# An encoder kernel on Trainium2: layer 1's gate projection by Strassen's seven block products

## The chip, the cores and the metric

The kernel runs on one core of one Trainium2 chip. A core has five engines that run side by side, each with its own queue of instructions: TensorE (PE, matrix products; its weight loads are listed apart as PEld), VectorE (DVE), ScalarE (ACT), GpSimd (POOL) and SyncE (SP, which here only issues DMAs). Data lies in DRAM, in SBUF (128 partitions) and in PSUM, into which TensorE writes. The metric is the device time of one execution in microseconds (us), and the median of several runs counts. The profile shows one execution.

## The reference: what is computed

A two-layer encoder on x of 1024 tokens x 1024 features, float32. Layer 0 is differential attention, layer 1 multi-head latent attention; the change touches layer 1. Each layer does

```python
h = _rmsnorm(x, norm_g[i]) * (1.0 + scale) + shift      # shift, scale, gate = silu(c) @ ada_w + ada_b
x = x + gate * y
```

and layer 1's `y`, with one input projection of 384 + 256 + 64 + 1024 columns, is

```python
proj = h @ w_in
q_a, c_kv, k_pe, z = jnp.split(proj, [384, 640, 704], axis=-1)
q = (_rmsnorm(q_a, q_a_norm_g) @ w_q_b)                  # 8 heads x (128 + 64)
kv = (_rmsnorm(c_kv, kv_a_norm_g) @ w_kv_b)              # 8 heads x (128 key + 128 value)
k_pe = _rope(k_pe, positions)
...                                                      # softmax attention per head
o = o.reshape(b, s, MLA_WIDTH) * jax.nn.silu(z)
return o @ w_out
```

`z`, the gate path, is the part whose matrix product changes: 1024 tokens x 1024 features by 1024 x 1024 weights. `q_a` (384 wide) and `c_kv` (256 wide) are the latents.

## The kernel before

**Numbers in two parts.** TensorE is fed a reduced float32 type (`F32R`). To keep float32 accuracy every operand is held as a high part (a rounded copy) and a low part (what is left), and each product is three matmuls into one PSUM bank (`mm3`, L177: high x high L178, high x low L179, low x high L180). An operand tile is 128x512; splitting one is a ScalarE copy and a GpSimd subtraction (`split_raw`, L214, lines L223 and L224, tiles `wh` and `wl`).

**Layer 1's input projection.** Its input h1 is kept transposed: 8 chunks of 128 features (`h1[k]`), each in two halves of 512 tokens, high and low. `group0` (L1166) makes them from the residual rows: transposes on TensorE, the high part on ScalarE, a float32 copy in a temporary and the low part on VectorE (`h_chunk`, L473). The projection is made in strips of 128 output columns. A strip is 2 halves x 8 chunks x 3 matmuls, and its weights are two 256 KB loads, each split in `split_raw`.

- Strip 0 is k_pe, with its rotation (`rope`, `kp_half`).
- Strips 1 to 3 are q_a, strips 4 and 5 c_kv (`lora`, L1223). `put` copies each half out of PSUM (`craw`), squares it (`csq`) and adds the squares up (`csum`, L1237). `norm` brings the sums onto partitions, takes the root on GpSimd (`rq_y`) and sends it through DRAM to all partitions (`bc_s`). `rest` scales (VectorE, L1251), copies the high part (ScalarE, L1254) and subtracts (GpSimd, L1255) into the tiles CQ and CK, which stay in SBUF until attention has used them.
- Strips 6 to 13 are z, one for each head (`z1_strip`, L1282). `silu_gate` (L701) makes z·(1 + tanh(z/2)) straight from PSUM, and the result goes to DRAM (`zS`).

Beside the z strips the modulation's gate of layer 1 is made: `gen_gate` (L438) loads eight 512 KB rows and reduces each in one VectorE operation (L428, in `mod_dot`). In the last z strip `load_wk` (L1304) loads and splits the value weights. Then `v1_tile` (L1314) makes the first half of the values, `store_v` (L353) splits each out of PSUM (L355 ScalarE, then VectorE) into one of three `v_hl` tiles and stores it (`vS`), and then `Stream` (L296) makes the heads' keys and queries (`kn`, `qn`, `qp`) from CK and CQ ahead of and beside attention (`attn1`, L1404).

**What sets the order.** Each engine runs its instructions in one fixed order. A planner chooses it when the program is built: instructions are taken in program order as far as what they need is thought to be ready. Python's order thus matters, and so do the lists that spread work: `Side` (L275) runs one entry at each tick, a tick being one chunk of a strip's loop, `norms` runs what is due at chunk `NORM_AT` = 4 of a half-strip, and `behind` ties an instruction to a place. Tiles with the same tag share buffers, and a new tile waits for the one that it replaces.

Of the kernel before, what the change touches and what calls it, by code (L numbers as in the profile page):

```python
# [78 lines left out]
def f32v(ap):  # L79
    return ap.bitcast(F32)  # L80
# [3 lines left out]
def trunk(ctx: ExitStack, tc: tile.TileContext, A, out):  # L84
# [388 lines left out]
    def h_chunk(l, xn4, k, dst, hp, sub=G, wide=False, act=False):  # L473
# [12 lines left out]
        tmp = hp.tile([P, n, P], F32, name="h32", tag="h32", bufs=2)  # L486
# [674 lines left out]
    w4 = []  # L1161
# [4 lines left out]
    def group0(gi, fulls):  # L1166
# [3 lines left out]
        def chunk(k):  # L1170
            if gi == 1:
                h1[k][1] = xt2k("h1h"), xt2k("h1l")
            h_chunk(1, fulls, k, h1[k][gi], p3x, V)
# [3 lines left out]
        side.add(*[lambda k=k: chunk(k) for k in range(KT)])  # L1177
# [13 lines left out]
    cqp = pool(stC, "cq", side="right")  # L1191
    CQ = [[(cqp.tile([P, HF], F32R, name=f"cqh{k}_{f}"), cqp.tile([P, HF], F32R, name=f"cql{k}_{f}")) for f in range(2)] for k in range(3)]
    CK = [[(cqp.tile([P, HF], F32R, name=f"ckh{k}_{f}"), cqp.tile([P, HF], F32R, name=f"ckl{k}_{f}")) for f in range(2)] for k in range(2)]
# [4 lines left out]
    st4 = ExitStack()  # L1198

    def kp_half(half, acc):  # L1200
        rot, fin = rope(wp, acc, half, 1.0)

        def g():
            rot()
            r = fin()
            hi = lr.tile([P, HF], F32R, name="kp_h", tag="kp_h", bufs=1)
# [5 lines left out]

    norms = []

    def half_and_norm(w, half, consume):

        for k, _ in enumerate(gen_half(w, h1, half, consume)):
            if k == NORM_AT:
                for f in norms[:]:
                    norms.remove(f)  # L1220
                    f()

    def lora(idx, dst, gvec, width, ws=None, first=None):  # L1223
# [3 lines left out]
        def put(i, half, acc):  # L1227
            t = lr.tile([P, HF], F32, name="craw", tag="craw", bufs=6)
# [5 lines left out]
            else:  # L1234
                s2 = lr.tile([P, HF], F32, name="csq", tag="csq", bufs=1)
# [3 lines left out]
        def norm(half):  # L1239
# [6 lines left out]
            _, rb = bcast_rows(lr, y, "cbc", 1)  # L1246

            def rest():
                for i in range(n):
# [3 lines left out]
                    hi, lo = dst[i][half]  # L1253
                    S.copy(hi, t)  # L1254
                    G.tensor_sub(lo, t, f32v(hi))  # L1255

            norms.append(rest)
# [11 lines left out]
    def first_halves(put):  # L1269

        g0 = kp_half(0, strip_half(w4[0], h1, 0))
# [3 lines left out]
        st3x.close()  # L1275
        g0()
        kp_half(1, strip_half(w4[0], h1, 1))()

    lora((1, 2, 3), CQ, qag, QL, w4[1], first_halves)
    lora((4, 5), CK, kvg, KVL)  # L1280

    def z1_strip(h, extra=None):  # L1282
        w = strip1(6 + h)
        if extra:
            extra()
        for half in range(2):
            def put(acc, half=half):
                gz = silu_gate(wp, acc)
# [338 lines left out]
```

## Time and profile before

| what | value |
| --- | --- |
| median of 3 runs | 1453.14 us (1454.03, 1447.42, 1453.14) |
| profiled execution | 1448.22 us |
| its span, first to last instruction | 1446.4 us |
| mean granted TensorE clock | 0.995 |
| instructions | 20456 |
| DMA traffic | 203.19 MB, mean 140 GB/s |
| z strips | 858.03 to 949.23 us of the span |

How to read it: busy time is the time in which an engine worked on instructions, and idle time of an engine that is not the bottleneck costs nothing. A row of a group gives line, engine, operation, output <- inputs, shapes and count, then busy us and mean ns of one, then the engine's idle us ahead of these and what ended it. A row of the timeline gives start, duration, engine, line and operation, with the idle time before it in brackets. A granted clock of 1.00 is TensorE's full speed.

### The profile page before, as it was taken

Reading aid. Unit: us, or ns where it says so; the run is one execution under the profiler, and the core shown is the slowest. Engines: PE = TensorE matmul, PEld = TensorE weight load, DVE = VectorE, ACT = ScalarE, POOL = GpSimd, SP = SyncE. Lnnn points to the kernel's source line nnn. Section 1 sums busy time; section 2 is a strip of 40 time slices with the busy share of each in tenths; the row PEclk is TensorE's granted clock in tenths of the full one; section 3 lists DMA queues with packets and bytes.
Section 4 is the critical chain, followed back from the end, with each engine's and each line's share of the span. In section 5 each row is a group of like instructions: output and inputs, shape, how many; then the busy total and the mean of one; then the engine's idle time right before and its main releaser. Section 6 shows DMA issues by size and latency. Waiting matters only on the chain.

```text
span 1446.4 us, 20456 instructions
## 1 busy us (share of the span) xinstructions
PE 1396.9 (97%) x7424; PEld 1167.0 (81%) x7424; DVE 858.4 (59%) x1272; ACT 710.5 (49%) x1258; POOL 605.0 (42%) x484
## 2 busy tenths in 40 slices
PE   5999999999999999998999999998999999999997
PEld 4778788888888887887787878787888888888886
DVE  6656777767777767677344445134555555555365
ACT  5522366656565665566343332234454554545342
POOL 4416164656564655453551264321141321412473
PEclk9999999999999999999999999999999999999999
DMA  9787823333333324137653127367242332345574
GB/s 327 234 248 234 256 66 97 87 103 81 101 97 88 98 81 110 63 95 262 229 171 124 38 69 239 110 189 204 77 104 77 110 99 76 105 136 175 172 238 149
DMA packets 128470, 203.19 MB, mean 140 GB/s; under 512 B 18289, under 2 KB 55281, under 8 KB 128369
## 3 DMA queue, kind: packets, MB, share of 16 engines
q1 hardware_dynamic: 128368, 201.89, 45.6%
q8 instruction: 58, 0.95, 0.3%
q14 instruction: 44, 0.35, 0.1%
HBM read 132.68 MB, written 45.56 MB: 123 GB/s over the span
## 4 chain that ended last, share of the span: by engine, by line
PE 77%; DMA 7%; DVE 6%; ACT 3%; POOL 3%; issue 2%; SPq 2%; ACTq 0%; DVEq 0%; POOLq 0%
PE s L1397 10%; PE acc L180 8%; PE acc L179 8%; PE acc L178 8%; PE tr L376 7%; PE s L767 7%; PE pv L179 4%; PE pv L178 4%; PE pv L180 4%; PE oacc L178 4%; PE oacc L179 4%; PE oacc L180 4%; DMA ada<-in_ada_g 2%; DMA wvr<-in_w_v 2%; DMA vS<-v_hl 1%
## 5 line engine op out<-in xcount | busy, mean ns | idle before, releaser
L378 ACT CAST pth<-tr 128x512 fp32r<-128x512 f32 x256 | 150.3, 587 | 283.6 <-PE tr L376 280.0
L393 DVE TENSOR_REDUCE nm<-s 128x1 f32<-128x1024 f32 x192 | 234.0, 1219 | 73.6 <-PE s L767 64.0
L379 DVE TENSOR_TENSOR ptl<-tr,pth 128x512 fp32r<-128x512 f32 x256 | 176.2, 688 | 150.2 <-ACT pth L378 149.9
L224 POOL TENSOR_TENSOR wl<-wraw,wh 128x512 fp32r<-128x512 f32 (+2 forms) x94 | 116.8, 1244 | 243.4 <-ACT wh L223 216.2
L395 ACT ACTIVATE e<-s,nm 128x1024 f32<-128x1024 f32 x128 | 143.7, 1122 | 28.1 <-DVE nm L393 27.6
L376 PE MATMUL tr<-ident,e 128*128 128x128 f32 x1024 | 154.6, 273 | 1.9 <-DVE ptl L379 1.7
L376 PEld LDWEIGHTS tr<-ident,e 128*128 128x128 f32 x1024 | 121.5, 140 | 42.8 <-DVE ptl L379 19.2
L178 PE MATMUL acc<-h0h,wh 128*128 128x512 f32 x360 | 150.0, 417 | 2.0 <-DVE v_hl L356 1.9
L178 PE MATMUL pv<-pth,vt 128*128 128x256 f32 x512 | 147.4, 288 | 0.0
L179 PE MATMUL pv<-ptl,vt 128*128 128x256 f32 x512 | 145.5, 284 | 0.0
L180 PE MATMUL pv<-pth,vt 128*128 128x256 f32 x512 | 144.6, 282 | 0.0
L180 PE MATMUL acc<-h0h,wl 128*128 128x512 f32 x360 | 142.2, 395 | 0.5 <-POOL wl L224 0.5
L179 PE MATMUL acc<-h0l,wh 128*128 128x512 f32 x360 | 141.4, 393 | 0.0
L1007 POOL TENSOR_TENSOR wol<-wor,woh 128x512 fp32r<-128x512 f32 x64 | 85.8, 1361 | 84.4 <-ACT woh L1006 79.4
L178 PEld LDWEIGHTS pv<-pth,vt 128*128 128x128 f32 x512 | 97.6, 191 | 3.0 <-ACT pth L378 0.4
L179 PEld LDWEIGHTS pv<-ptl,vt 128*128 128x128 f32 x512 | 97.7, 191 | 2.6
L180 PEld LDWEIGHTS pv<-pth,vt 128*128 128x128 f32 x512 | 97.7, 191 | 0.1
L325 POOL TENSOR_TENSOR rp_sw<-rp_sw,sinT 128x512 f32<-128x512 f32 x42 | 55.2, 1314 | 80.6 <-DMA rp_sw<-rp_raw 77.6
L767 PE MATMUL s<-ks,qa 128*128 128x512 f32 x256 | 82.2, 402 | 3.5 <-DVE e L775 3.1
L775 DVE SCALAR_TENSOR_TENSOR e<-s,z,e 128x1024 f32<-128x1024 f32 x64 | 82.1, 1283 | 2.1
L223 ACT CAST wh<-wraw 128x512 fp32r<-128x512 f32 (+2 forms) x94 | 55.2, 587 | 55.8 <-PE acc L179 38.5
L320 POOL TENSOR_TENSOR rp_r<-rp_raw,cosT 128x512 f32<-128x512 f32 x38 | 49.4, 1302 | 78.5 <-ACT rp_raw L315 50.8
(469 smaller groups left out, 3281.7 us busy)
## 6 DMA issues: line engine op xcount, KB each, us to landing
wraw<-in_w_s SPq DMA_DIRECT2D x76, 256.0 KB, 2.8
ada<-in_ada_ss SPq DMA_DIRECT2D x32, 512.0 KB, 6.1
vS<-v_hl SPq DMA_DIRECT2D x32, 512.0 KB, 4.9
vt<-vS SPq DMA_DIRECT2D x32, 512.0 KB, 4.0
wor<-in_w_out SPq DMA_DIRECT2D x64, 256.0 KB, 3.9
rp_sw<-rp_raw SPq DMA_DIRECT2D x168, 64.0 KB, 2.0
bc_s<-bc_d SPq DMA_DIRECT2D x34, 256.0 KB, 4.0
ada<-in_ada_g SPq DMA_DIRECT2D x16, 512.0 KB, 5.2
```

What stands on the lines that cost most here:

```text
L178: PE.matmul(psum, ah, bh, start=first, stop=False)
L179: PE.matmul(psum, ah, bl, start=False, stop=False)
L180: PE.matmul(psum, al, bh, start=False, stop=last)
L224: sub = (V if pair_of else G).tensor_sub(l_[:, :n], raw[:, :n], f32v(h_[:, :n]))
L376: PE.transpose(tr[:, j, :], p[:, kt * P : (kt + 1) * P], ident)
L378: mk["S"] = S.copy(pth[kh][:, :, dst], tr).ins
L379: mk["V"] = V.tensor_sub(ptl[kh][:, :, dst], tr, f32v(pth[kh][:, :, dst])).ins
L393: mk["V"] = V.reduce_max(nm, s_ps, axis=AX.X, negate=True).ins
L395: mk["S"] = S.activation(e, s_ps, AF.Exp, bias=nm, scale=1.0, accum_out=zs).ins
L767: PE.matmul(s_ps[:, kc * HF : (kc + 1) * HF], src[:, c, ql], KS[h][kc][:, c, :], start=fst, stop=not fst)
L1007: in_turn(G.tensor_sub(lo, raw, f32v(hi)))
L1397: PE.matmul(s_ps[:, kc * HF : (kc + 1) * HF], lhs, rhs(kc), start=i == 0, stop=i == 4)
```

## The change

The z product is made block by block, by Winograd's form of Strassen's scheme. For two strips (2p and 2p + 1) the weights are four blocks (two strips x two halves of the features, 256 KB each) and h1 four blocks (two halves of the features x two halves of the tokens, each four chunks). Seven block products of 4 chunks x 3 matmuls replace eight.

- **Combinations of h1** (`combos`): T1 to T4, four chunks each. h1's second half is kept in float32 for it (`h1f`, written by `h_chunk` in the place of its temporary), and the first half is taken as high + low. Each is made by VectorE, then split by a ScalarE copy and a GpSimd subtraction (`split_t`). They run from the side list, one at every second tick, and `half_and_norm` and the second half of strip 0 tick now. The chunks of the second half come in the order 0, 4, 1, 5 and so on.
- **Combinations of the weights** (`z_weights`): four VectorE operations for a pair, and seven splits in place of four. The loads (`z_fetch`) are issued after products 3 and 5 of the pair before.
- **Products** (`z_pair`): each ends in one or two VectorE additions out of PSUM (the first in a ScalarE copy), and the gate (`gate_out`) is made from the sum in SBUF.
- **Room**: 24 tiles (`ut`) hold h1f and T1 to T3 (T2 in tiles that h1f gives up), in the place where CQ and CK stood. The latents' parts go to DRAM (`cS`, 20 stores of 256 KB) and come back in the last pair: CK after product 4, CQ after product 5, behind the first value weights. Small temporaries move to shared tags.
- **Moved**: the modulation's gate goes from beside the z strips into attention (`gate_steps`), in halves of 512 columns. The second value weights are loaded between pairs 1 and 2, the first `w_qr` strip is loaded ahead of the value tiles and split after the fourth.

```diff
-        tmp = hp.tile([P, n, P], F32, name="h32", tag="h32", bufs=2)
+        tmp = f32.rearrange("p (j q) -> p j q", j=4) if f32 is not None else hp.tile([P, n, P], F32, name="h32", tag="h32", bufs=2)
...
-    w4 = []
+    w4, h1f = [], {}
...
-            h_chunk(1, fulls, k, h1[k][gi], p3x, V)
+                h1f[k] = ut(f"h1f{k}", dt=F32)
+            h_chunk(1, fulls, k, h1[k][gi], p3x, V, f32=h1f[k] if gi else None)
...
-        side.add(*[lambda k=k: chunk(k) for k in range(KT)])
+        side.add(*[lambda k=k: chunk(k) for k in ((0, 4, 1, 5, 2, 6, 3, 7) if gi else range(KT))])
...
-    cqp = pool(stC, "cq", side="right")
-    CQ = [[(cqp.tile([P, HF], F32R, name=f"cqh{k}_{f}"), cqp.tile([P, HF], F32R, name=f"cql{k}_{f}")) for f in range(2)] for k in range(3)]
-    CK = [[(cqp.tile([P, HF], F32R, name=f"ckh{k}_{f}"), cqp.tile([P, HF], F32R, name=f"ckl{k}_{f}")) for f in range(2)] for k in range(2)]
+    up = pool(stC, "u", side="right")
...
+    def ut(name, spare=False, dt=F32R):
+        return up.tile([P, HF], dt, name=name, tag="us" if spare else "u", bufs=4 if spare else 20)
...
+    TC = {}
+    cS = dr.tile([5, 2, 2, P, HF], F32, name="cS")
...
+    def rpt(name, dt=F32):
+        return wp.tile([P, HF], dt, name=name, tag="rp", bufs=6)
...
+    def h1q(q, half):
+        return [h1[4 * q + k][half] for k in range(4)]
+
+    def split_t(n, k, t, dst):
+        TC.setdefault(n, {})[k] = dst
+        S.copy(dst[0], t)
+        G.tensor_sub(dst[1], t, f32v(dst[0]))
...
+    def combos():
+
+        t1d, t3d = [None] * 4, [None] * 4
+        for n, d_ in ((3, t3d), (1, t1d)):
+            for k in range(4):
+                d_[k] = [ut(f"t{n}{x_}", n == 1 and k > 1) for x_ in "hl"]
+        for k in range(4):
+            (ah, al), (bh, bl) = h1[k][0], h1[k + 4][0]
+            c_, d_ = h1f[k], h1f[k + 4]
+            t1 = tmp4("t1")
+            V.tensor_sub(t1, c_, f32v(ah))
+            V.tensor_sub(t1, t1, f32v(al))
+            split_t(1, k, t1, t1d[k])
+            yield
+            t3_ = tmp4("t3")
+            V.tensor_sub(t3_, d_, c_)
+            split_t(3, k, t3_, t3d[k])
+            yield
+            t2 = tmp4("t2")
+            V.tensor_sub(t2, d_, t1)
+            split_t(2, k, t2, (ut("t2h"), ut("t2l")))
+            yield
+            t4 = tmp4("t4f")
+            V.tensor_sub(t4, f32v(bh), t2)
+            V.tensor_add(t4, t4, f32v(bl))
+            pl, tag = (p4, "t4") if k < 2 else (h1p, "whl")
+            split_t(4, k, t4, [pl.tile([P, HF], F32R, name="t4" + x_, tag=tag, bufs=4) for x_ in "hl"])
+            yield
+
...
         for k, _ in enumerate(gen_half(w, h1, half, consume)):
+            side.tick()
...
-            _, rb = bcast_rows(lr, y, "cbc", 1)
...
+            _, rb = bcast_rows(wp, y, "rp", 6)
...
-                    hi, lo = dst[i][half]
+                    pl, tag = (wp, "rp") if dst else (p4, "zraw")
+                    hi = pl.tile([P, HF], F32R, name="c_h", tag=tag, bufs=6)
                     S.copy(hi, t)
-                    G.tensor_sub(lo, t, f32v(hi))
...
+                    G.tensor_sub(t.bitcast(F32R), t, f32v(hi))
+                    his.append(hi)
+                norms.append(store)
...
+            def store():
+                for i in range(n):
+                    SP.dma_start(cS[dst + i, half, 0], f32v(his[i]))
+                    SP.dma_start(cS[dst + i, half, 1], craw[i][half])
...
+        p4 = pool(st4, "p4")
...
-        kp_half(1, strip_half(w4[0], h1, 1))()
-
-    lora((1, 2, 3), CQ, qag, QL, w4[1], first_halves)
-    lora((4, 5), CK, kvg, KVL)
...
-    def z1_strip(h, extra=None):
-        w = strip1(6 + h)
-        if extra:
-            extra()
...
-            def put(acc, half=half):
-                gz = silu_gate(wp, acc)
-                SP.dma_start(zS[h, half], gz)
-            half_and_norm(w, half, put)
-
-    z1_strip(0)
+        cg = combos()
+        for _ in range(16):
+            side.add(lambda: next(cg), None)
+        accs = []
+        for _ in gen_half(w4[0], h1, 1, accs.append):
+            side.tick()
+        kp_half(1, accs[0])()
+
+    p4 = None
+    lora((1, 2, 3), 0, qag, QL, w4[1], first_halves)
...
+    def z_fetch(p, parts):
+        for m, f in parts:
+            raw = p4.tile([P, HF], F32, name="zraw", tag="zraw", bufs=6)
+            SP.dma_start(raw, A["w_s1"][6 + 2 * p + m, f])
+            zraw.append(raw)
+
+    lora((4, 5), 3, kvg, KVL)
+    side.flush()
+    z_fetch(0, ((0, 0), (0, 1), (1, 0), (1, 1)))
...
+    def z_weights():
+
+        for _ in range(NH // 2):
+            a11, a12 = zraw[:2]
+            yield split_raw(a11, 4)
+            yield split_raw(a12, 4)
+            a21, a22 = zraw[2:4]
+            del zraw[:4]
+            s1 = p4.tile([P, HF], F32, name="zs1", tag="zraw", bufs=6)
+            V.tensor_add(s1, a21, a22)
+            V.tensor_sub(a21, a11, a21)
+            V.tensor_sub(a11, s1, a11)
+            V.tensor_sub(a12, a12, a11)
+            for t in (a11, a21, s1, a22, a12):
+                yield split_raw(t, 4)
...
+    def gate_out(h, half, c_, dst):
+
+        th = wst.tile([P, HF], F32, name="zth", tag="gz", bufs=3)
+        S.activation(th, c_, AF.Tanh, scale=0.5)
+        V.scalar_tensor_tensor(out=dst, in0=th, scalar=1.0, in1=c_, op0=ALU.add, op1=ALU.mult)
+        SP.dma_start(zS[h, half], dst)
...
+    zw = z_weights()
+    zq = [next(zw), next(zw)]
...
+    def product(rhs):
+
+        hi, lo = zq.pop(0)
+        zq.append(next(zw, None))
+        acc = bank("acc", "zacc")
+        for k in range(4):
+            mm3(acc, hi[k], lo[k], *rhs[k], k == 0, k == 3)
+            ticks[0] += 1
+            if ticks[0] % 8 == NORM_AT:
+                run_norms()
+        return acc
+
+    def z_pair(p, late=lambda i: None):
+        more = p + 1 < NH // 2
+        u = rpt("zu")
+        S.copy(u, product(h1q(0, 0)))
+        acc = product(h1q(1, 0))
+        c_ = rpt("z11")
+        V.tensor_add(c_, acc, u)
+        gate_out(2 * p, 0, c_, c_)
+        V.tensor_add(u, product(TC[2]), u)
+        late(0)
+        if more:
+            z_fetch(p + 1, ((0, 0), (0, 1)))
+        acc = product(TC[3])
+        u3 = rpt("zu3")
+        V.tensor_add(u3, acc, u)
+        late(1)
+        acc = product(TC[1])
+        c_ = rpt("z22")
+        V.tensor_add(c_, acc, u3)
+        V.tensor_add(u, acc, u)
+        gate_out(2 * p + 1, 1, c_, c_)
+        late(2)
+        if more:
+            z_fetch(p + 1, ((1, 0), (1, 1)))
+        V.tensor_add(u3, product(TC[4]), u3)
+        gate_out(2 * p + 1, 0, u3, u3)
+        V.tensor_add(u, product(h1q(1, 1)), u)
+        gate_out(2 * p, 1, u, u)
...
-    p4 = pool(st4, "p4")
...
-    c2, c_fin = load_c(p4, p4.tile([P, D], F32, name="cth", tag="ada", bufs=2))
-    c_fin()
-    gates = gen_gate(1, lambda src: mod_load(src, p4, 2), c2)
-    next(gates)
...
-    def load_wk(fh, wpool):
...
             SP.dma_start(raw, A["w_v1"][k, fh])
-            h_ = wpool.tile([P, HF], F32R, name="wvh", tag="wv1", bufs=4)
-            l_ = wpool.tile([P, HF], F32R, name="wvl", tag="wv1", bufs=4)
+            h_, l_ = [pv1.tile([P, HF], F32R, name="wv" + x_, tag="wv1", bufs=4) if fh else ut("wv" + x_, True) for x_ in "hl"]
...
-    for h in range(1, NH):
-        next(gates)
-        z1_strip(h, lambda: [load_wk(fh, wpool) for fh, wpool in enumerate((p4, pv1))] if h == NH - 1 else None)
+    CK, CQ = [[None, None] for _ in range(2)], [[None, None] for _ in range(3)]
+
+    def load_ck(dst, n0, order):
...
+            dst[i][half] = ut("ckh"), ut("ckl")
+            for j, t in enumerate(dst[i][half]):
+                SP.dma_start(f32v(t), cS[n0 + i, half, j])
+
+    def late_z(i):
+        if i == 1:
+            load_ck(CK, 3, [(k, half) for half in range(2) for k in range(2)])
+        if i == 2:
+            load_wk(0)
+            load_ck(CQ, 0, [(i, half) for half in range(2) for i in range(3)])
...
+    z_pair(1)
+    load_wk(1)
+    z_pair(2)
+    z_pair(3, late_z)
+    st4.close()
+    p4 = pool(st4, "p4v")
+    kraw = fetch_strip([A["w_qr"][0]], [3])
     for tt in range(NT):
         v1_tile(tt, 0, p4)
+        if tt == 3:
+            wkn0 = split_strip(kraw)
...
+    def gate_steps():
+
+        for i in range(2):
+            SP.dma_start(cg2[i], A["c"][:, i * HF : i * HF + HF].to_broadcast([P, HF]))
...
+        for i in range(2):
+            with behind("S"):
+                S.activation(gw[i], cg2[i], AF.Tanh, scale=0.5)
...
+        for i in range(2):
+            with behind("V"):
+                V.scalar_tensor_tensor(out=cg2[i], in0=gw[i], scalar=1.0, in1=cg2[i], op0=ALU.add, op1=ALU.mult)
+        for j in range(KT):
+            yield
+            for i in range(2):
+                SP.dma_start(gw[i], A["ada_g1"][j, :, i * HF : i * HF + HF])
...
+            js = slice(j, j + 1)
+            for i in range(2):
+                with behind("V"):
+                    mod_dot(gw[i], part("ada_bg1")[:, js] if i == 0 else gcol1[:, js], gcol1[:, js], cg2[i])
...
-    stream1 = Stream(gen_strips(items))
+    stream1 = Stream(gen_strips(items, wkn0))
...
+    ap2 = pool(st5, "attn1b")
     for h in range(NH - 1):
-        attn1(h, lambda i: FILL1[i])
+        attn1(h, lambda i: FILL1[i], lambda i: next(gate1, None))
         while late_q:
```

43 lines of the change are left out of this document (32 added, 11 removed).

## The prediction

> **What bounds the kernel now.** I read the page first (busy shares, the clock, the chain of work that ended last), then the table by stage for the stretch that the change rewrites, then TensorE's waits there.
>
> ```profile
> PE 1396.9 (97%) x7424; PEld 1167.0 (81%) x7424; DVE 858.4 (59%) x1272; ACT 710.5 (49%) x1258; POOL 605.0 (42%) x484
> PE 77%; DMA 7%; DVE 6%; ACT 3%; POOL 3%; issue 2%; SPq 2%; ACTq 0%; DVEq 0%; POOLq 0%
> ```
>
> TensorE is busy for 97% of the span and carries 77% of the chain, so in general a matmul removed is time gained. By stage (columns: stretch, its length, busy us of PE, PEld, DVE, ACT and POOL with instruction counts, granted clock, DMA share, GB/s):
>
> ```profile
> 808.00:858.00 50.00, 48.87 (x224) 39.95 (x224) 16.39 (x19) 17.04 (x31) 25.78 (x19) 1.00 0.21 58
> 858.00:949.23 91.23, 89.69 (x394) 72.79 (x393) 29.93 (x42) 22.18 (x38) 32.13 (x25) 1.00 0.48 155
> 949.23:985.00 35.77, 31.35 (x132) 25.24 (x131) 13.56 (x20) 14.46 (x26) 11.96 (x10) 0.96 0.80 223
> 1030.00:1300.00 270.00, 269.53 (x1625) 230.57 (x1624) 144.25 (x191) 138.21 (x251) 76.63 (x62) 1.00 0.36 102
> ```
>
> The first row is the rest of layer 1's narrow strips (k_pe and the latents), the second the eight gate strips, the third the first values (v) and the first keys and queries, the fourth attention. TensorE fills the first two. But in the first, VectorE and GpSimd together are already busy 42.2 of 50 us, and that is where the change puts its combinations. TensorE's waits between 786 and 1345 us (what waited, for what: us in all, times, longest):
>
> ```profile
> PE vps L178 <- DVE qn_l L1349: 4.4, 1, 4.4
> PE acc L180 <- POOL wl L224: 1.5, 1, 1.5
> ```
>
> **The change, part by part.** *Fewer matmuls.* Before, 8 strips x 2 halves x 8 blocks x 3 are 384 matmuls; after, 4 pairs x 7 products x 4 x 3 are 336. The pitch comes from the starts of two half-strips, 48 matmuls apart:
>
> ```profile
> 869.98 0.39 PE L178 MATMUL acc<-h_0h,wh 128*128 128x512 f32 x1
> 881.04 0.39 PE L178 MATMUL acc<-h_0h,wh 128*128 128x512 f32 x1
> ```
>
> 11.06 us for 48, so 0.2304 us each: **-11.1 us**. The 1.5 us wait for a GpSimd split above belongs to a strip whose weights were late; the pairs fetch theirs at other times, and I let it go: **-1.5**.
>
> *The sixteen combinations.* Per k they are 6 VectorE operations with both inputs in SBUF (t1 two, t3 one, t2 one, t4 two), 4 ScalarE copies and 4 GpSimd subtractions: 24, 16 and 16 in all. They are put on the ticks of four half-strips, one every second tick, so all stand in program order ahead of strip 3's weight splits on GpSimd. Their prices are the pitches of like operations run back to back:
>
> ```profile
> 816.11 0.69 DVE L329 TENSOR_TENSOR rp_r<-rp_r,rp_sw 128x512 f32<-128x512 f32 x1 [7.60 <-POOL rp_sw L325]
> 816.72 0.69 DVE L1237 TENSOR_TENSOR csum<-csum,csq 128x512 f32<-128x512 f32 x1
> 810.33 1.30 POOL L224 TENSOR_TENSOR wl<-wraw,wh 128x512 fp32r<-128x512 f32 x1 [5.60 <-PE acc L180]
> 811.59 1.30 POOL L320 TENSOR_TENSOR rp_r<-rp_raw,cosT 128x512 f32<-128x512 f32 x1
> ```
>
> 0.61 us on VectorE and 1.26 on GpSimd: 24 x 0.61 + 16 x 1.26 = 14.6 + 20.2 = 34.8 us. On two engines that would lie side by side; whether it may is the disputed point. The trace has both engines at it at 853:
>
> ```profile
> 853.02 1.28 POOL L1255 TENSOR_TENSOR cql<-craw,cqh 128x512 fp32r<-128x512 f32 x1
> 853.30 1.55 DVE L1237 TENSOR_TENSOR csum<-csum,csq 128x512 f32<-128x512 f32 x1 [2.65 <-ACT csq L1236]
> 854.26 1.71 POOL L224 TENSOR_TENSOR wl<-wraw,wh 128x512 fp32r<-128x512 f32 x1
> ```
>
> The addition that takes 0.69 elsewhere starts during a GpSimd subtraction and ends at 854.85, 0.55 after that one's end; the GpSimd operation that starts meanwhile takes 1.71 instead of 1.30, as if it had begun when the addition ended. So they take turns, and I add them instead of laying them side by side. The Trainium skill, "SBUF — State Buffer", section "Who interferes with whom", says just that: a VectorE instruction with two SBUF inputs contends with a GpSimd instruction that reads SBUF, and whichever holds the shared ports first blocks the other for its whole length. By that rule the sum stands; without it, it is that of rival 2.
>
> What is free of the 50 us? The stretch's own groups, at their prices alone:
>
> ```profile
> L224 POOL TENSOR_TENSOR wl<-wraw,wh 128x512 fp32r<-128x512 f32 x8 | 10.7, 1340 | 18.2 <-ACT wh L223 12.6 <-PE acc L180 5.6
> L1255 POOL TENSOR_TENSOR cql<-craw,cqh 128x512 fp32r<-128x512 f32 x6 | 9.7, 1637 | 3.7 <-ACT cqh L1254 3.7
> L165 POOL TENSOR_TENSOR rq_y<-c_w,mhalf 128x4 f32<-128x4 f32 x3 | 3.0, 1008 | 3.1 <-DVE c_w L1244 3.1
> L1237 DVE TENSOR_TENSOR csum<-csum,csq 128x512 f32<-128x512 f32 x5 | 4.7, 945 | 14.1 <-ACT csq L1236 14.1
> ...
> L1251 DVE SCALAR_TENSOR_TENSOR craw<-craw,vec,bc_s x10: 1129/1150/2181, 838.6 to 870.6; 128x512 f32<-128x512 f32 x10
> ```
>
> GpSimd: 8 splits, 6 latent subtractions and 2 rope products x 1.26, and 3 x 1.01: 23.2. VectorE: 6 craw x 1.13, 5 csum x 0.61, three further 0.6 operations and 0.8 of casts: 12.4. Together 35.6, free 14.4. Of 34.8 that leaves **+20.4** in which strips 3 to 5 wait for their splits. Bounds: nothing (rival 1), and the whole 34.8 if the free time falls where no input is ready. I take the subtraction, since the rows at 853 are this very pair of operations.
>
> *The first gate pair.* Left over behind 858 are 4 ckl x 1.26, 4 craw x 1.13, 1.0 and 0.6: 11.1. A pair's weights take 7 splits x 1.26 and 4 additions, and its gates 4 operations with both inputs in SBUF now: 7 x 1.26 + 8 x 0.61 = 13.7. Together 24.8, against 7 x 12 x 0.2304 = 19.4 us of matmuls: **+5.4**. Later pairs have 13.7 in 19.4, hidden. The 28 PSUM additions have one SBUF input; at 0.685 (the gate operation below, of the same kind) they are 19.2 us of VectorE in 80, hidden too.
>
> ```profile
> L706 DVE SCALAR_TENSOR_TENSOR gz<-zth,acc 128x512 f32<-128x512 f32 x15 | 10.2, 685 | 35.7 <-ACT zth L705 35.5
> L428 DVE CUSTOM_DVE_ANT_0 ada<-ada,c,vec 128x1024 f32<-128x1024 f32 x8 | 11.6, 1450 | 10.8 <-DMA ada<-in_ada_g 10.8
> ```
>
> *ScalarE.* 16 copies at 0.6 are 9.6 us, in a stretch with 17.04 of 50 busy, and 12 more splits in the gate stage with 22.18 of 91: nothing, unless a copy stands behind an operation that waits for a combination.
>
> *Latents to DRAM and back.* The 20 stores of 256 KB fall where the DMA share is 0.21 and 0.48: nothing. The reload is late on purpose: CK's after product 4 of the last pair, CQ's and wk0's after product 5, on SP's queue ahead of the v stores.
>
> ```profile
> 880.00:900.00 20.00, 20.00 (x89) 16.22 (x88) 10.54 (x16) 4.06 (x7) 7.41 (x6) 1.00 0.78 265
> ...
> 958.85 0.59 ACT L355 CAST v_hl<-vps 128x512 fp32r<-128x512 f32 x1 [1.26 <-DMA vS<-v_hl]
> ```
>
> 5.24 MB at 265/0.78 = 340 GB/s is 15.4 us. CK is asked for 3.5 products (9.7 us) before the stage's end, so the transfer ends about 6 us behind it; the first v store came 3 us behind it. From there the v tiles are paced by their stores: the copy at 958.85 waited for one. So about 3 to 6, **+4** (bounds 0, if the stores slip between the reloads, and 8, if every one queues behind them).
>
> *The gate's modulation* (the 11.6 us above) moves into attention, as 16 half-width operations. VectorE is busy 144.25 of 270 us there: nothing, bound +2 where one stands ahead of a softmax step. Taking it out of the gate stage gains nothing, since VectorE set nothing there.
>
> *The clock.* A long stop of TensorE costs more than itself:
>
> ```profile
> 908.13 0.50 PE L180 MATMUL acc<-h_4h,wl 128*128 128x512 f32 x1 [1.54 <-POOL wl L224]
> 908.46 0.40 PE L178 MATMUL acc<-h_5h,wh 128*128 128x512 f32 x1
> ...
> 982.71 0.79 PE L178 MATMUL vps<-wvh,ckh 128*128 128x512 f32 x1 [4.42 <-DVE qn_l L1349]
> 983.30 0.63 PE L179 MATMUL vps<-wvl,ckh 128*128 128x512 f32 x1
> 983.72 0.63 PE L180 MATMUL vps<-wvh,ckl 128*128 128x512 f32 x1
> ...
> 985.00:990.00 5.00, 5.00 (x15) 3.94 (x14) 0.92 (x2) 0.59 (x1) 0.00 (x0) 0.61 0.99 280
> ```
>
> After 4.42 us idle the matmuls come 0.43 us apart and the clock is 0.61 until near 990, after 1.54 us idle they don't. Some 15 matmuls at 0.2 more, 3.3 with the first: **+3.3** once, since a 20 us wait spread over strips 3 to 5 has at least one such stop in it. The Trainium skill, "TensorE: Matmul & The Clock Gate", Part 1, puts the bound at one idle window of about 3.4 us and the return at another such window of work; the two stops here lie on either side of it.
>
> **Sum**, against the profiled execution (1448.22 us, span 1446.4 with 1.8 around it): -11.1 - 1.5 + 20.4 + 5.4 + 4 + 3.3 = **+20.5**, 1468.7. The median of the runs, 1453.14, lies 4.9 above that execution, so the forecast is **1473.6 us**.
>
> **The rivals.**
> 1. *The other side: faster.* VectorE and GpSimd don't hinder each other and the weight splits reach GpSimd ahead of the combinations, which then use spare time only. That leaves -12.6 + 4 = -8.6: 1444.5. It decides at strip 3, whose weights must be there when it starts:
>
> ```profile
> 818.68 1.28 POOL L224 TENSOR_TENSOR wl<-wraw,wh 128x512 fp32r<-128x512 f32 x1 [2.60 <-ACT wh L223]
> ...
> 820.73 0.39 PE L178 MATMUL acc<-h_0h,wh 128*128 128x512 f32 x1
> ```
>
> The split ended at 819.96, so 0.8 us later is too late. For it: GpSimd's own load, 25.78 + 20.2 of 50, fits. Against: the rows at 853, and the order in the program. 0.16.
>
> 2. *GpSimd's queue alone.* No turn-taking, but strip 3's splits stand behind the combinations: from 808, 16 x 1.26 + 2 rope products 2.5 + another split 1.3 end at 832.0, 11.3 after 820.73. -12.6 + 11.3 + 3.3 + 4 = +6.0: 1459.1. For it: the queue is in order. Against: 853 again. 0.14.
>
> 3. *The pairs stall too.* Each later pair's chain (three dependent additions, a ScalarE copy of 0.6, a split: 1.8 + 0.6 + 1.3 = 3.7) starts only when its second fetch has landed, and isn't covered: 3 x 3.7 = 11.1 more, 1484.7. For it: the fetch waits for tiles that the pair before gives up late. Against: 5.7 us of slack in each pair. 0.14.
>
> **How the numbers follow.** Forecast 0.56, rivals 0.16, 0.14, 0.14. A measurement of this kernel can tell some 0.5% (7.3 us) from no change: the first rival falls under 1445.9 (faster 0.16), the second within (same 0.14), the forecast and the third above 1460.4 (slower 0.70). The range reaches from 1444, which takes in the overload's bound of nothing, to 1488, which takes in the third rival and the overload at its other bound (14.4 more): 1444 to 1488.
>
> **What would show it.** Right: TensorE idle by some 20 us between 820 and 860, mostly on GpSimd's wl; combination operations of VectorE and GpSimd at 1.3 to 2 us instead of 0.69 and 1.30 where they meet; 336 matmuls at 0.23 in the gate stage; one stretch with a granted clock under 0.8 in strips 3 to 5; v stores waited for at the stage's end. Wrong: VectorE operations at 0.69 beside busy GpSimd, or strips 3 to 5 starting back to back, or a wait in the gate stage or in attention larger than any priced here.

## The result, and the profile after

The changed kernel takes 1472.93 us (median of 4 runs, 1471.80 to 1477.85) where the kernel before takes 1453.59 in the same comparison: a ratio of 1.0148 (95% interval 1.0111 to 1.0185), slower by 19.3 us. A second comparison on another chip gave 1.0186 (1.0169 to 1.0203). The forecast was 1473.6. Its terms don't come out as well as its sum, and most of this part is about that.

The page of the changed kernel, first its busy shares (they answer to the first line quoted in the prediction):

```profile
span 1470.0 us, 20657 instructions
PE 1396.5 (95%) x7376; PEld 1163.9 (79%) x7376; DVE 926.9 (63%) x1357; ACT 729.6 (50%) x1291; POOL 655.2 (45%) x512
```

TensorE has 48 matmuls less (7424 to 7376) and is as long busy as before (1396.9 to 1396.5 us): what it saved it gave back at a slow clock, and its idle time grew. The table by stage shows where. The stretches are strip 3, strips 4 and 5, the first gate pair, the other three, and from there to attention's first transposition; the columns are those of the prediction's table.

```profile
819.62:856.59 36.97, 18.19 (x57) 13.87 (x56) 26.32 (x21) 10.18 (x19) 28.71 (x19) 0.70 0.09 29
856.59:881.29 24.70, 24.70 (x114) 20.37 (x112) 10.72 (x10) 9.26 (x17) 13.38 (x10) 0.97 0.61 197
881.29:908.52 27.23, 22.54 (x94) 17.61 (x92) 17.44 (x20) 9.56 (x17) 19.55 (x14) 0.94 0.57 170
908.52:968.20 59.68, 58.72 (x253) 46.95 (x252) 36.81 (x49) 21.01 (x35) 32.29 (x24) 1.00 0.44 150
968.20:1017.30 49.10, 41.87 (x165) 32.49 (x164) 17.55 (x25) 18.39 (x33) 13.59 (x12) 0.93 0.82 240
```

And two of the same stretches in the kernel before, strip 3 and the way from the last gate strip to attention's first transposition:

```profile
820.73:832.74 12.01, 12.01 (x58) 9.89 (x57) 1.75 (x3) 3.32 (x6) 3.53 (x3) 1.00 0.19 55
949.23:994.40 45.17, 40.75 (x166) 32.74 (x165) 16.86 (x24) 17.32 (x31) 11.96 (x10) 0.92 0.79 220
```

Strip 3 is the case: 36.97 us instead of 12.01, the clock at 0.70. Of the 25.0 us more, TensorE is idle for 18.8 (36.97 - 18.19), and for the same 48 matmuls it is busy 6.2 us longer (18.19 against 12.01), at the slow clock. VectorE and GpSimd are busy for 55 us together in 37; time in which one is held up by the other counts as busy here. TensorE's waits in the changed kernel from 808 to 1005 us:

```profile
PE cps L1295 <- DVE csum L1290: 10.1, 2, 7.1
PE acc L178 <- ACT wh L223: 8.6, 3, 3.8
PE acc L180 <- POOL wl L224: 8.3, 2, 7.9
PE zacc L180 <- POOL wl L224: 2.6, 4, 1.2
PE acc L178 <- DVE v_hl L356: 1.9, 1, 1.9
```

Three engines make it wait, one after the other: in strip 3 it waits 3.8 us for ScalarE's copy of a weight, 7.9 for GpSimd's subtraction and 7.1 for VectorE's sum of squares (18.8 together). What the first and the third wait for stands on ScalarE's queue behind copies of combinations, which wait for VectorE:

```profile
825.20 0.62 ACT L1227 CAST t3h<-t 128x512 fp32r<-128x512 f32 x1 [0.57 <-DVE t L1248]
825.73 0.61 ACT L223 CAST wh<-wraw 128x512 fp32r<-128x512 f32 x1
...
848.25 0.62 ACT L1227 CAST t4h<-t4f 128x512 fp32r<-128x512 f32 x1 [2.25 <-DVE t4f L1257]
848.78 0.59 ACT L1289 ACTIVATE csq<-acc 128x512 f32<-128x512 f32 x1
```

The stage lengths of all kernels, from the starts of the first matmul of each strip or pair ("to output projection" is from the end of the gate stage to the first matmul of the output projection, which takes in attention). All in us of one profiled execution each; the two rows of the changed kernel show by how much such lengths vary:

| kernel | strip 3 starts | strip 3 | strip 4 | strip 5 | gate stage (first pair) | to output projection | span |
| --- | --- | --- | --- | --- | --- | --- | --- |
| before | 820.7 | 12.0 | 11.9 | 13.4 | 91.2 | 388.4 | 1446.4 |
| changed | 819.6 | 37.0 | 12.7 | 12.0 | 86.9 (27.2) | 393.0 | 1470.0 |
| changed, again | 821.2 | 36.9 | 12.0 | 12.6 | 87.2 (27.5) | 391.7 | 1470.4 |
| e1_psum_operand | 821.3 | 23.9 | 12.8 | 12.0 | 86.8 (27.1) | 393.4 | 1459.1 |
| e2_subs_vector | 819.3 | 11.1 | 25.9 | 22.8 | 86.1 (23.2) | 393.4 | 1468.0 |
| e3_spread | 820.2 | 24.2 | 11.9 | 24.4 | 81.4 (21.8) | 392.9 | 1463.7 |
| e4_in_psum | 819.7 | 11.1 | 13.4 | 23.2 | 86.4 (23.3) | 393.4 | 1456.7 |
| e5_no_combos | 829.1 | 15.4 | 11.9 | 12.6 | 87.3 (27.7) | 392.7 | 1457.9 |
| e6_early_fetch | 819.1 | 37.0 | 12.1 | 13.1 | 84.4 (23.5) | 393.9 | 1468.6 |
| e8_reload | 821.6 | 34.6 | 12.8 | 13.1 | 86.3 (26.8) | 390.4 | 1467.0 |
| e7_psum_early | 821.4 | 11.1 | 13.6 | 16.3 | 85.8 (24.0) | 390.5 | 1447.6 |
| e10_gate_psum | 817.4 | 11.1 | 13.7 | 17.2 | 83.1 (22.6) | 390.7 | 1442.1 |
| e11_latents_vector | 821.1 | 11.1 | 13.6 | 18.3 | 81.0 (22.8) | 390.1 | 1443.6 |
| e12_every_fifth | 821.2 | 13.0 | 11.9 | 15.6 | 80.5 (20.8) | 390.6 | 1441.1 |

### The profile page after: what moved, and what is told of

The parts are those of the page before. It is cut to its first block, busy times and chain, and to the rows that moved or that the text cites. A ratio compares the mean times of both kernels' runs of the same rounds, so it can differ in the third digit from the quotient of the medians.

```text
span 1470.0 us, 20657 instructions
## 1 busy us (share of the span) xinstructions
PE 1396.5 (95%) x7376; PEld 1163.9 (79%) x7376; DVE 926.9 (63%) x1357; ACT 729.6 (50%) x1291; POOL 655.2 (45%) x512
## 5 line engine op out<-in xcount | busy, mean ns | idle before, releaser
L224 POOL TENSOR_TENSOR wl<-wraw,wh 128x512 fp32r<-128x512 f32 (+2 forms) x78 | 102.9, 1321 | 204.7 <-ACT wh L223 193.4
L376 PEld LDWEIGHTS tr<-ident,e 128*128 128x128 f32 x1024 | 121.6, 140 | 43.3 <-DVE ptl L379 18.3
L767 PE MATMUL s<-ks,qb 128*128 128x512 f32 x256 | 80.9, 395 | 0.0
```

What stands on the lines that cost most here:

```text
L224: sub = (V if pair_of else G).tensor_sub(l_[:, :n], raw[:, :n], f32v(h_[:, :n]))
L376: PE.transpose(tr[:, j, :], p[:, kt * P : (kt + 1) * P], ident)
L767: PE.matmul(s_ps[:, kc * HF : (kc + 1) * HF], src[:, c, ql], KS[h][kc][:, c, :], start=fst, stop=not fst)
```

## The experiments

The kernel before took 1444.9 to 1453.6 us (medians) on the chips used, so times are compared by their ratio to it on the same chip, and stages by the table. Two theories for the stop in strip 3 were set against each other. A is the forecast's: VectorE with two SBUF inputs and GpSimd take turns. B is rival 2: only the order of GpSimd's queue makes the weight splits late.

**e1_psum_operand.** The second input of the combinations' VectorE operations becomes a bank of PSUM.

```diff
-            V.tensor_sub(t1, c_, f32v(ah))
-            V.tensor_sub(t1, t1, f32v(al))
+            V.tensor_sub(t1, mp, f32v(ah))
+            V.tensor_sub(t1, mp, t1)
...
```

> The 24 VectorE operations of the combinations keep their number and their output, but one of the two inputs is now a constant bank of PSUM (so the values of T1 to T4 are left out); the 16 GpSimd subtractions stay. Theory A (VectorE with two SBUF inputs and GpSimd take turns): the combinations' VectorE operations come back to 0.7 us beside a busy GpSimd, the 14.6 us of VectorE no longer add to GpSimd's, and some 9 to 15 us of the overload go: 1458 to 1464 us. Theory B (the order of GpSimd's queue alone makes the splits late): the queue is the same, 1470 to 1476 us.

Measured: 1458.59 us, ratio 1.0090 (1.0073 to 1.0108). The figure lies in A's band only because this chip is faster (the kernel before took 1445.78); by ratio it would be 1467 where the forecast was made, 3 us over the band. Against the changed kernel it is 8 to 14 us less by ratio and 10.9 by span, and strip 3 falls from 37.0 to 23.9. B expected no change and falls. Single rows show why; first the timeline of the changed kernel (rows of VectorE and GpSimd):

```profile
814.94 1.77 DVE L1252 TENSOR_TENSOR t<-h1f,t 128x512 f32<-128x512 f32 x1 [2.45 <-POOL t1l L1228]
816.12 1.74 POOL L1228 TENSOR_TENSOR t2l<-t,t2h 128x512 fp32r<-128x512 f32 x1
...
818.33 1.78 DVE L1243 TENSOR_TENSOR t<-h1f,h_2h 128x512 f32<-128x512 f32 x1
819.52 1.75 POOL L320 TENSOR_TENSOR rp_r<-rp_raw,cosT 128x512 f32<-128x512 f32 x1
820.03 1.78 DVE L1257 TENSOR_TENSOR t4f<-t4f,h_5l 128x512 f32<-128x512 f32 x1
```

then that of e1_psum_operand:

```profile
815.09 1.31 POOL L224 TENSOR_TENSOR wl<-wraw,wh 128x512 fp32r<-128x512 f32 x1
815.42 0.69 DVE L1258 TENSOR_TENSOR t4f<-cz,t 128x512 f32<-128x512 f32 x1
816.14 0.69 DVE L1259 TENSOR_TENSOR t4f<-cz,t4f 128x512 f32<-128x512 f32 x1
816.35 1.31 POOL L320 TENSOR_TENSOR rp_r<-rp_raw,cosT 128x512 f32<-128x512 f32 x1
```

With two SBUF inputs both engines slow to one operation each in 1.70 us; with one in PSUM (`cz`) they run side by side at their own 0.69 and 1.31. The Trainium skill ("SBUF — State Buffer", "Who interferes with whom") says of both cases what these rows show: two SBUF inputs contend with a GpSimd instruction that reads SBUF, one doesn't. Strip 3 is still 11.9 us longer than before: TensorE waits 1.7 us for a split and 7.1 for the sums, and the slow clock takes 3.1 (15.15 us busy against 12.01). The square of the last sum stands on ScalarE's queue behind four copies of combinations, the first of which waits 4.17 us for VectorE. That these 11.9 us are queues alone isn't shown, since other operations with two SBUF inputs (those of k_pe, the sums) still meet GpSimd there.

**e2_subs_vector.** The combinations' low parts on VectorE.

```diff
-        G.tensor_sub(dst[1], t, f32v(dst[0]))
+        V.tensor_sub(dst[1], t, f32v(dst[0]))
```

> The low parts of T1 to T4 are subtracted on VectorE instead of GpSimd: 40 VectorE operations of 0.61 us, none on GpSimd. Theory A (turns): 24.4 us of two-input work in place of 34.8 beside the 35.6 that are there, so 10 us over 50 in place of 20: about 1462 us (1458 to 1467). Theory B (GpSimd's queue alone): the splits are free of the combinations, the whole stop before the gate pairs goes: 1447 to 1453 us.

Measured: 1469.34 us, ratio 1.0163 (1.0148 to 1.0178). Both theories missed: B by all of it, and A's sum (34.8 us becoming 24.4) too. Strip 3 is free, but strips 4 and 5 take 25.9 and 22.8. Its timeline:

```profile
834.18 9.48 POOL L224 TENSOR_TENSOR wl<-wraw,wh 128x512 fp32r<-128x512 f32 x2 [11.15 <-ACT wh L223]
834.60 0.68 DVE L1244 TENSOR_TENSOR t<-t,h_3l 128x512 f32<-128x512 f32 x1
...
840.62 0.68 DVE L1228 TENSOR_TENSOR t4l<-t4f,t4h 128x512 fp32r<-128x512 f32 x1
842.48 0.80 PE L180 MATMUL acc<-h_4h,wl 128*128 128x512 f32 x1 [7.64 <-POOL wl L224]
```

VectorE runs on without a gap at a pitch of 0.60, and two splits on GpSimd (one row here) take 9.48 us instead of 2.5: the first takes 8.24, ending 1.1 us after VectorE's last operation, the second 1.27. TensorE waits 7.64 for the first. The engines don't take turns here: GpSimd is shut out until VectorE has run dry. Adding the operations up was too simple a price.

**e3_spread.** One combination at every fifth tick.

```diff
-            side.add(lambda: next(cg), None)
+            side.add(lambda: next(cg), *[None] * 4)
```

> The changed kernel with the sixteen combinations on every fifth tick instead of every second, so over strips 0 to 5 and not 0 to 2. Theory A (turns): VectorE and GpSimd have the same work to share in the stretch; the long stop in strip 3 is divided over strips 3 to 5, but the gate pairs start about as late (within 5 us of 881 us), 1466 to 1475 us. Theory B (order alone): each weight split waits for one combination at most, 1.3 us, so nearly all of the 23 us go and 1450 to 1455 us are left.

Measured: 1465.17 us, ratio 1.0138 (1.0115 to 1.0161). The gate pairs start at 880.7, where the changed kernel has 881.3, with the stop divided over strips 3 and 5: A's expectation, not B's (by ratio 1474 us where the forecast was made). The longest wait of strip 5, 9.5 us, is again for the sum of squares, so queues have a part in it. The gain lies in the first pair (21.8 instead of 27.2 us).

**e4_in_psum.** The same values, made in PSUM.

```diff
-            V.tensor_sub(t1, c_, f32v(ah))
-            V.tensor_sub(t1, t1, f32v(al))
-            split_t(1, k, t1, t1d[k])
+            a = bank("tr", "cA")
+            S.copy(a, c_)
...
+            V.tensor_sub(a, a, f32v(ah))
+            V.tensor_sub(a, a, f32v(al))
+            split_p(1, k, a, t1d[k])
...
+        S.copy(dst[0], t)
+        V.tensor_sub(dst[1], t, f32v(dst[0]))
```

> The same values, made in PSUM: ScalarE copies the kept float32 chunk into a bank, every VectorE operation of a combination reads that bank and one SBUF tile, and the low part is subtracted on VectorE from the bank. 40 VectorE operations of 0.6 to 0.7 us, 20 ScalarE copies, none on GpSimd, none with two SBUF inputs. Theory A (turns): nothing of it contends with GpSimd; VectorE has 26 us more in a stretch where it has room for them, so most of the 20.4 + 3.3 us go and 1448 to 1453 us are left, with rows of 0.7 us beside a busy GpSimd. Theory C (VectorE's own queue is what is full: sums of squares and scaling stand behind the combinations): VectorE has more operations than in the changed kernel, so 1465 us or more.

Measured: 1459.14 us, ratio 1.0088 (1.0066 to 1.0109): by ratio some 13 us over the upper end of A's expectation, and 13.3 us of span under the changed kernel. Strip 3 takes 11.1 us, less than before the change, so the whole 25 us there were the combinations, by their contention and by their place on the queues. VectorE had 16 operations more than in the changed kernel and was not too full in strip 3, so C falls there, though by ratio (1466 us where the forecast was made) the time alone would fit it. But strip 5 now takes 23.2 instead of 12.0 us. TensorE's two longest waits from 808 to 960 us, and ScalarE's rows in front of the first:

```profile
PE cps L1299 <- DVE csum L1294: 4.7, 1, 4.7
PE zacc L178 <- ACT wh L223: 3.9, 1, 3.9
```

```profile
848.88 0.59 ACT L1286 COPY craw<-acc 128x512 f32<-128x512 f32 x1 [0.68 <-DMA cS<-craw]
...
855.53 0.62 ACT L1312 CAST c_h<-craw 128x512 fp32r<-128x512 f32 x1 [1.01 <-DVE craw L1308]
856.05 0.59 ACT L1293 ACTIVATE csq<-acc 128x512 f32<-128x512 f32 x1
```

What is late next is the latents' path: a copy out of PSUM waits for a store to `cS` (the parking), the square of the next strip stands on ScalarE's queue behind a copy that waits for VectorE, and TensorE waits 4.7 us for the sum, then 3.9 us for the first pair's weights. Contention has a part here too: the scaling that the copy waits for has two SBUF inputs and takes 2.14 us beside a GpSimd subtraction, 1.13 alone.

**e5_no_combos.** Copies in place of the combinations.

```diff
+            for n, t, dd in ((1, c_, t1d[k]), (3, d_, t3d[k]), (2, f32v(bh), None), (4, f32v(bh), None)):
...
+                S.copy(dd[0], t)
+                S.copy(dd[1], t)
```

> The combinations' VectorE and GpSimd operations are left out: T1 to T4 are filled by 32 ScalarE copies of other tiles (their values are left out), and the products, the parked latents and the reload stay as they are. By the forecast's sum, 20.4 + 3.3 us go and 5.4 in the first pair and 4 at the reload stay: about 1449 us (1446 to 1453). If the stop before the gate pairs were the latents' new path (temporaries in shared tags, stores) and not the combinations, the time would stay above 1462 us.

Measured: 1458.44 us, ratio 1.0080 (1.0055 to 1.0105). It doesn't decide what it was meant to. The time lies between the two expectations (by ratio, 1465 where the forecast was made, above 1462), but ScalarE is busy 18.93 of the 21 us from 808 to 829, mostly with the 32 copies, weight copies stand behind them, and strip 3 starts 8 us late. Its first pair takes 27.7 us as in the changed kernel, so that excess doesn't need the combinations.

**after_again, e6_early_fetch, e8_reload, e7_psum_early** ran on one chip.

> The changed kernel once more, so that the others of this set are compared with it on the same chip: ratio to the kernel before 1.015 (1.011 to 1.0185), strip 3 taking 37 us again.

Measured: 1474.52 us, ratio 1.0186, strip 3 36.9 us: just over the end of the expected band.

e6 issues the first pair's loads ahead of strip 5:

```diff
+            if ahead and i == n - 1:
+                ahead()
...
-    lora((4, 5), 3, kvg, KVL)
+    lora((4, 5), 3, kvg, KVL, ahead=lambda: z_fetch(0, ((0, 0), (0, 1), (1, 0), (1, 1))))
```

> The changed kernel with one edit: the first pair's four weight loads are issued ahead of strip 5 instead of behind it. By the forecast's step (the first pair has 24.8 us of two-input work in 19.4 us of matmuls) the loads have no say: the first pair keeps its 27 us and the time stays within 2 us of the changed kernel's. By the rival (the first copy of the pair waits 3.9 us for its load, and the sums of the last strip stand behind it on ScalarE's queue) the first pair falls to 21 or 22 us and the time by 4 to 6 us.

Measured: 1471.78 us, ratio 1.0166 (1.0147 to 1.0185), 2.7 us under the changed kernel, which the intervals don't set apart. The first pair falls from 27.5 to 23.5, the second rises from 21.0 to 22.3. The cause shows in the changed kernel's rows, in ScalarE's:

```profile
880.26 0.62 ACT L223 CAST wh<-zraw 128x512 fp32r<-128x512 f32 x1 [3.87 <-DMA zraw<-in_w_s]
882.39 0.62 ACT L223 CAST wh<-zraw 128x512 fp32r<-128x512 f32 x1 [1.51 <-DMA zraw<-in_w_s]
882.92 0.58 ACT L1282 COPY craw<-acc 128x512 f32<-128x512 f32 x1
883.40 0.60 ACT L1289 ACTIVATE csq<-acc 128x512 f32<-128x512 f32 x1
```

and in VectorE's:

```profile
883.82 1.16 DVE L1372 TENSOR_TENSOR zs<-zraw 128x512 f32<-128x512 f32 x1 [4.37 <-DMA zraw<-in_w_s]
...
887.20 0.68 DVE L1290 TENSOR_TENSOR csum<-csum,csq 128x512 f32<-128x512 f32 x1
```

Two copies wait for loads, and the last strip's square stands behind them; then the sum stands behind the pair's four weight combinations on VectorE, the first of which had waited 4.37 us for its load. TensorE waited 3.1 us for that sum. The rival is right on the place, and got half of what it promised.

e8 brings the latents back one product earlier (T2 and CK share eight tiles of their own):

```diff
-        if i == 1:
+        cq = [(i, half) for half in range(2) for i in range(3)]
+        if i == 0:
             load_ck(CK, 3, [(k, half) for half in range(2) for k in range(2)])
+        if i == 1:
+            load_ck(CQ, 0, cq[:4])
         if i == 2:
             load_wk(0)
-            load_ck(CQ, 0, [(i, half) for half in range(2) for i in range(3)])
+            load_ck(CQ, 0, cq[4:])
```

> The changed kernel with one edit: the 24 tiles are allotted so that CK comes back after product 3 of the last pair, four of CQ's six after product 4 and the rest after product 5, each one product (2.8 us) earlier than in the change. By the forecast's step (the reload's backlog, 4 us) up to 2.8 us of the waits between the last pair and attention go. If those waits come from the value stores alone, nothing changes there.

Measured: 1470.40 us, ratio 1.0156 (1.0139 to 1.0173). The stretch after the gate stage falls from 393.0 or 391.7 to 390.4 us: 1.3 to 2.6, as expected; of TensorE's waits there the one for a value tile (1.9 or 2.3 us) is gone. The rest of its 4.1 us is in strip 3 (34.6), which the other allotment of tiles shifted too.

e7 has e4, e6 and e8 together.

> Three edits together: the combinations in PSUM as in e4_in_psum, the first pair's loads ahead of strip 5 as in e6_early_fetch, and the reload of the latents one product earlier as in e8_reload. If the costs are separate they add: e4_in_psum's 14 us of span, 4 to 6 and 2 off the changed kernel, so 20 to 22 us off and about the time of the kernel before (ratio 0.998 to 1.003). If the latents' stores and their chain through ScalarE and VectorE are what is late next, strip 5 keeps 20 us or more and the ratio stays at 1.006 to 1.009.

Measured: 1448.40 us, ratio 1.0003 (0.9991 to 1.0016), 26 us under the changed kernel. By span it is 22.8 us less, where the three alone took off 13.3, 1.8 and 3.4 (18.5; the first of them on another chip). Single profiles make such a sum rough, but strip 5, 23.2 us in e4_in_psum and 16.3 here, shows where the others are worth more once the first stop is gone.

**e10_gate_psum** leaves the gates' last addition in PSUM, **e11_latents_vector** also moves the latents' subtractions to VectorE, and **e12_every_fifth** also spreads the combinations.

```diff
-        V.tensor_add(c_, acc, u)
-        gate_out(2 * p, 0, c_, c_)
+        V.tensor_add(acc, acc, u)
+        gate_out(2 * p, 0, acc, rpt("z11"))
...
-                    G.tensor_sub(t.bitcast(F32R), t, f32v(hi))
+                    V.tensor_sub(t.bitcast(F32R), t, f32v(hi))
...
-            side.add(lambda: next(cg), None)
+            side.add(lambda: next(cg), *[None] * 4)
```

> e7_psum_early with the last addition of each gate block left in its PSUM bank, so that the gate operation has one SBUF input (16 operations of the gate stage less with two). If taking turns still costs TensorE in the first two pairs of e7_psum_early (24.0 and 23.2 us against 19.3 for the others), they fall by 1 to 3 us each and the time by 2 to 5 us, to a ratio of 0.996 to 0.999. If those pairs wait for the four weight combinations and the latents alone, the ratio stays at 1.000.

Measured: 1444.20 us, ratio 0.9992 (0.9979 to 1.0006). The first two pairs fall from 24.0 and 23.2 to 22.6 and 21.9 us, as expected if contention still costs there; the time alone doesn't set it apart from e7_psum_early.

> e10_gate_psum with the latents' low parts (10 operations) subtracted on VectorE instead of GpSimd: each scaling and subtraction of a latent then runs at 1.13 and 0.61 us with no GpSimd subtraction beside it, the chain that the sums of strip 5 stand behind gets about 3 us shorter for each half, and strip 5 falls from 16.3 us to about 13.5 (before: 13.35). 2 to 5 us less than e10_gate_psum. If the chain is paced by the transfer of the root instead, nothing changes.

Measured: 1443.03 us, ratio 0.9985 (0.9975 to 0.9996). A miss: strip 5 takes 18.3 us (17.2 in e10_gate_psum), and the wait for the sum stays at 3.6 (3.8). VectorE's queue is longer now: the square is done at 858.4, and its sum starts at 859.58, behind a subtraction and a scaling of the latents. What gained was the second pair (19.5 instead of 21.9 us).

> e11_latents_vector with the combinations on every fifth tick instead of every second. On VectorE and ScalarE the sums of squares of strip 3 and the scaling of the latents then stand ahead of the last combinations instead of behind them, and TensorE's small products for the root come some 30 matmuls (7 us) earlier. If the wait for the sums in strip 5 (3.6 us, and the slow clock behind it) comes from that queueing, strip 5 falls from 18.3 us to 13 to 15 and the time by 3 to 5 us: 1438 to 1441 us where the kernel before takes 1445, ratio 0.995 to 0.997. If it comes from the latents' stores and the transfer of the root on SyncE's queue, the wait stays and the ratio is 0.9985 as before.

Measured: 1444.17 us, ratio 0.9978 (0.9963 to 0.9992). Strip 5 falls to 15.6 us, between the two expectations. TensorE's waits from 808 to 945 us are now

```profile
PE cps L1299 <- DVE csum L1294: 3.1, 2, 2.4
PE zacc L180 <- POOL wl L224: 1.1, 1, 1.1
```

This last kernel has the lowest ratio of the set, though it isn't set apart from e11_latents_vector: by ratio it is 25 to 30 us under the changed one, and 0.2% faster than the one before, with an interval that leaves out 1. The 11 us of the seven products are thus worth some 3 us (the interval reaches from 1 to 5) once their combinations don't contend.

## Why the prediction was right, point by point

Against the profiled execution the forecast was +20.5 us; measured are +23.6 of both span and execution (1448.22 to 1471.80), and +19.3 of the medians. That the forecast median, 1473.6, lies within 1 us of the measured 1472.93 is luck: the sum was 3 us too small, and the 4.9 us by which it put the median above the profiled execution were 1.1 for the changed kernel. By stage:

- *Up to the gate pairs*: forecast +20.4 and +3.3 for the clock, 23.7; measured 881.29 - 858.03 = 23.3. The size is right, and e4_in_psum, where strip 3 takes 11.1 us, shows that the combinations are the cause. The mechanism is right in part. e1_psum_operand takes the combinations' contention alone away and 13.1 of strip 3's 25.0 us go; the other 11.9 are for the most part in-order queues and the slow clock behind their stops, ScalarE's queue more than GpSimd's, where rival 2 had priced GpSimd's at 11.3. ScalarE was forecast as nothing "unless a copy stands behind an operation that waits for a combination", and that is what happened. So the sign "mostly on GpSimd's wl" came out for 7.9 of the 18.8 us only. The forecast took the two as exclusive, and both were at work. The step "they take turns, and I add them" failed in e2_subs_vector, where adding gave 10 us and GpSimd was shut out instead. One of the signs of being wrong, VectorE at 0.69 beside a busy GpSimd, showed from 808 to 813 us of the changed kernel too, but there GpSimd was held up for longer than its turn, not spared (last section). That free time absorbs 14.4 us was a guess that happened to fit.
- *The gate stage*: forecast -11.1 - 1.5 + 5.4 = -7.2; measured 86.9 - 91.2 = -4.3. The matmuls' term holds: the last two pairs take 19.3 us for 84 matmuls, 0.230 each. The 1.5 us that was let go came back as 2.6 (the zacc row): 1.6 in the first pair, 1.0 in the second. The first pair's excess over two strips of before (858.03 to 881.04) is 27.2 - 23.0 + 2.8 = 7.0 us, with 2.8 for the 12 matmuls that it has less; the forecast had 5.4, and put it to overload. Four of them were the late loads and the sum behind them, of which the second pair took 1.2 back (e6_early_fetch). The second pair, forecast as hidden, took 1.7 us more than the later ones.
- *The reload*: forecast +4; measured 49.10 - 45.17 = +3.9 in this profile, but +1.4 in the second profile of the changed kernel (after_again, 46.5), and e8_reload, earlier by a product, gets back 1.3 to 2.6. The step told is there: the first value store is issued 5.5 us into the stage, behind the last reload, instead of 3.0, and the value copy that waits for a store starts at 11.6 instead of 7.8. But its cost to TensorE comes out elsewhere. The 4.4 us stop of before is gone; TensorE waits 1.9 us for a value tile and 3.7 for the first key weights, whose load now stands on SyncE's queue behind eight value stores. The kernel before:

```profile
947.77 0.33 SPq L202 DMA_DIRECT2D wraw<-in_w_kn  x1
957.00 0.59 ACT L355 CAST v_hl<-vps 128x512 fp32r<-128x512 f32 x1 [2.79 <-DMA vS<-v_hl]
```

and the changed one:

```profile
973.68 14.95 SPq L358 DMA_DIRECT2D vS<-v_hl  x8
979.77 0.59 ACT L355 CAST v_hl<-vps 128x512 fp32r<-128x512 f32 x1 [1.00 <-DMA vS<-v_hl]
988.73 0.65 SPq L202 DMA_DIRECT2D wraw<-in_w_kn  x1
```

- *The gate in attention*: forecast nothing, bound +2; from attention's first transposition to the end the change takes 452.7 us, its second profile 454.0, and before 452.0. So the bound, not the forecast, is what the second profile shows. It isn't VectorE's operations that TensorE waits for, but the load of `c`: ScalarE waits 2.35 us for it (3.12 in the second profile), a softmax copy stands behind, and TensorE waits 0.94 us (1.72). No run tests this alone.

```profile
1027.23 0.63 ACT L1496 ACTIVATE gwh<-c2h 128x512 f32<-128x512 f32 x1 [2.35 <-DMA c2h<-in_c]
```

- *The clock*: forecast +3.3 once; strip 3 ran at 0.70 for all its 37 us and had three stops. By TensorE's busy time it cost 6.2 us there, and the waits were 18.8 where 20.4 were forecast: the two terms missed in opposite directions. (Strip 3's 25.0 us are 1.7 more than the 23.3 by which the gate pairs start late: strip 3 starts 1.1 us earlier than before, and strips 4 and 5 together take 0.6 less.)

The rivals: the first (faster) fell at the place that it named, strip 3's weights. The second fell as the whole account, but queues are a part of it. The third fell: the last two pairs take 19.3 us.

Left open: what decides whether VectorE and GpSimd alternate (814 to 828 us in the changed kernel) or GpSimd waits until VectorE stops (e2_subs_vector). A gap on VectorE isn't needed: at 839.81 us of the changed kernel a subtraction on GpSimd started during one VectorE operation, VectorE's next was issued without a gap at 840.20, and the subtraction took 1.61 us all the same. No run varied this alone.

## What to carry to other kernels

Here fewer matmuls paid only once what feeds them no longer held up other engines: look at the stage where the extra additions run, and sum up the operations of VectorE with two SBUF inputs and all of GpSimd's together, not each engine's share. An operand that is put in PSUM by an idle ScalarE takes an operation out of that sum. Then look at what waits on the in-order queues behind the added copies, since each wait that was removed here uncovered another: the sum of squares, the first loads, the gates.

## What was not expected of the hardware

GpSimd was shut out for long. In the changed kernel, as in e2_subs_vector, one split took 5.28 us instead of 1.30 while VectorE ran seven operations without a gap:

```profile
808.20 0.68 DVE L1252 TENSOR_TENSOR t<-h1f,t 128x512 f32<-128x512 f32 x1
808.37 5.28 POOL L224 TENSOR_TENSOR wl<-wraw,wh 128x512 fp32r<-128x512 f32 x1 [15.92 <-ACT wh L223]
...
811.80 0.69 DVE L1248 TENSOR_TENSOR t<-h1f,h1f 128x512 f32<-128x512 f32 x1
```

VectorE kept its 0.69 all the while. In the alternating stretch both engines lost, and a pair took 1.70 us, a little under the sum of their pitches (1.87).
